# A decoder trunk on one core: the low part of each weight tile formed by an accumulating DMA instead of VectorE

## The chip, the core and the metric

The kernel runs on 1 core of one Trainium2 chip. The metric is the device time of one execution in microseconds (us); a kernel's time is the median of its runs. The engines are named as the profile names them: PE (TensorE matmul), PEld (its weight load), DVE (VectorE), ACT (ScalarE), POOL (GpSimd) and SP (SyncE, which issues DMAs here).

## What is computed

One inference step of a two-layer decoder trunk, for one prompt of 512 tokens and 8 samples of 8 tokens, which share the weights. All is float32, 1024 channels wide. In short:

```python
# layer 0: RMSNorm -> h @ w_in_e -> GLU + causal conv (31) + LayerNorm + swish, and sliding-window attention
#          -> concat @ w_out_e, added to x
# layer 1: RMSNorm -> h @ w_in_o -> causal conv (4), Mamba-2 SSD scan, gate, grouped RMSNorm -> y @ w_out_o, added to x
# behind each layer, the feed-forward part:
def conv_ffn(h, hist, w_gate, w_up, conv_w, conv_b, w_down):
    gate = h @ w_gate
    padded = jnp.concatenate([hist, gate], axis=1)
    gc = causal_dwconv(padded, conv_w, conv_b)
    y = (jax.nn.silu(gc) * (h @ w_up)) @ w_down
    return y, padded[:, -(FFN_CONV_WIDTH - 1):]
```

The outputs are the new x of both groups and the new states (convolution histories, key/value windows, SSM states).

## The kernel before

The 512 prompt tokens and 64 sample tokens stand side by side as 576 columns; channels lie on the 128 partitions. Activations are tiles of 128x576, and each product is made in two halves of 288 columns (`HALF`).

**Three products for one.** The matmuls run on operands of type float32r. To keep float32 accuracy, each operand is split into a high part, which is the value rounded to float32r, and a low part, which is the value minus the high part. `mm3` (line 152) then adds three products for each block of 128x128 weights: high weight by high activation (line 158), high weight by low activation (line 159), low weight by high activation (line 160).

**Weight tiles.** The weights come as tiles of 128x1024 (512 KB), a few as 128x896 and one as 128x256; there are 215. `weights_load` (line 137) takes a tile `wr` and loads it by a DMA on SP's queue. `weights` (line 143) then takes tiles `wh` and `wl`, makes the high part on ACT (line 148) and the low part on DVE (line 149, `wr - wh`). Each of the three tags has 3 buffers, so a tile's slot is used again three weight tiles later: `wr` once the low part has been formed, `wh` and `wl` once PE has done its last matmul with them. A 1024-wide tile feeds 48 matmuls (8 blocks, 3 products, 2 halves).

**The stages.** `mix0` is layer 0's mixer, `mix1` layer 1's with the scan `ssd`, and `ffn` comes behind each. `units` (line 243) runs a product with its evacuation per weight tile; `out_proj` (line 259) the projections that are added to x. In `ffn` weight tiles follow each other with little else on PE; in `mix0` and `mix1` PE also does transposes, attention, and small scan matmuls, while DVE and ACT do convolutions and exponentials (line 734 is a DVE step of layer 1's convolution; `acb` are tiles of decays that a DMA spreads over the partitions; line 995 is a GpSimd product on the SSM state `h`).

**What sets the order.** The tile framework schedules the program while it is built: each engine has one queue, filled in an order that the scheduler chooses from priorities and its own estimate of when inputs are there, and each instruction then waits on semaphores on the chip. GpSimd's queue before holds only small things: clearing and copying of a few columns of history (lines 296, 297, 304, 305, 722, 723, 730, 731) and the 32 products of line 995. No DMA is issued by GpSimd.

Of the kernel before, what the change touches and what calls it, by code (L numbers as in the profile page):

```python
# [6 lines left out]
F32 = mybir.dt.float32  # L7
# [3 lines left out]
ADD, SUB, MUL, MAX, MIN = ALU.add, ALU.subtract, ALU.mult, ALU.max, ALU.min  # L11
# [37 lines left out]
class Builder:  # L49
# [93 lines left out]
    def weights(self, src, n):  # L143
        nc = self.nc
        raw = self.pre.pop(0) if self.pre else self.weights_load(src, n)
        hi = self.wp.tile([P, 1024], F32R, tag="wh", bufs=3, name="wh")
        lo = self.wp.tile([P, 1024], F32R, tag="wl", bufs=3, name="wl")
        nc.scalar.activation(hi[:, :n], raw[:, :n], AF.Copy)  # L148
        nc.vector.tensor_tensor(lo[:, :n], raw[:, :n], hi[:, :n].bitcast(F32), op=SUB)  # L149
        return hi, lo  # L150

    def mm3(self, out, w, blocks, xs, sl, m=P):
# [1114 lines left out]
```

## Time and profile before

| | us |
|---|---|
| median of 2 runs | 1621.99 (1621.31 to 1622.68) |
| the profiled execution's own time | 1617.26 |
| its span in the trace | 1615.5 |
| PE busy | 1588.7 (98%) |
| PEld busy | 1504.8 (93%) |
| DVE busy | 1026.3 (64%) |
| ACT busy | 696.5 (43%) |
| POOL busy | 109.4 (7%) |

How to read it: the span is cut from the first to the last instruction of the traced execution, and its own time lies 1.8 us above it. Busy time is what an engine's instructions take; PE's matmuls are pipelined, so that one has a length of about 300 ns though the next starts 130 ns later. The share of an engine is a mean over stages with different limits, and what a change is worth is read from the stage where it falls. Idle time in the profile is put down to what ended it. "SPq" and the like are an engine's queue, where DMAs are issued.

### The profile page before, as it was taken

What the parts mean: (1) busy time and instruction counts of PE and PEld (TensorE: products, weight loads), DVE (VectorE), ACT (ScalarE), POOL (GpSimd) and SP (SyncE); (2) the same over time, 40 slices, a digit from 0 to 9 for tenths busy, and PEclk for the clock granted to TensorE, in tenths of its full rate; (3) what the DMA queues carried; (4) which work ended last, traced back from release to release, by engine and by line L of the source; (5) the groups of instructions that cost most, each with busy time, mean ns of one, the idle gap of its engine ahead of it and who ended that gap; (6) DMA issues with size and microseconds to landing.
All of it is one profiled execution on the core that took longest, in us unless ns stands there. A gap on an engine that the chain in (4) does not pass through costs nothing.

```text
span 1615.5 us, 28735 instructions
## 1 busy us (share of the span) xinstructions
PE 1588.7 (98%) x11704; PEld 1504.8 (93%) x11704; DVE 1026.3 (64%) x1847; ACT 696.5 (43%) x1333; POOL 109.4 (7%) x322
## 2 busy tenths in 40 slices
PE   8999999999999999999999999999899999999999
PEld 8996699999999999998997998998799999999999
DVE  7898677654365355578796676676776653554552
ACT  7248654322122122378766556557352221221220
POOL 0000001000000000010301101101110000000000
PEclk9999999999999999999999999999899999999999
DMA  7222022222222222224335325234222222222222
GB/s 229 71 73 69 1 66 90 80 91 79 80 90 70 93 87 76 83 72 141 132 82 166 102 70 176 92 97 156 97 69 89 91 80 79 92 71 87 92 80 76
DMA packets 63633, 150.05 MB, mean 93 GB/s; under 512 B 18558, under 2 KB 19582, under 8 KB 63502
## 3 DMA queue, kind: packets, MB, share of 16 engines
q1 hardware_dynamic: 63502, 148.23, 28.8%
q8 instruction: 92, 1.51, 0.4%
q14 instruction: 39, 0.32, 0.1%
HBM read 133.86 MB, written 14.34 MB: 92 GB/s over the span
## 4 chain that ended last, share of the span: by engine, by line
PE 89%; DVE 5%; ACT 4%; DMA 2%; issue 1%; POOL 0%; SPq 0%; DVEq 0%; ACTq 0%
PE mm L158 25%; PE mm L160 25%; PE mm L159 25%; DVE cconv L734 1%; DMA acb<-acd 1%; PE yp L974 1%; ACT wh L148 1%; PE pst L923 1%; PE po L602 1%; PE sc L581 1%; PE pt L180 1%; PE pyo L987 1%; PE yp L972 1%; PE mm L524 1%; PE pr L191 1%
## 5 line engine op out<-in xcount | busy, mean ns | idle before, releaser
L158 PE MATMUL mm<-hh,wh 128*128 128x288 f32 (+1 forms) x2288 | 680.6, 298 | 8.4 <-ACT wh L148 7.7
L160 PE MATMUL mm<-hh,wl 128*128 128x288 f32 x2288 | 679.8, 297 | 0.1
L159 PE MATMUL mm<-hl,wh 128*128 128x288 f32 (+1 forms) x2288 | 677.9, 297 | 0.0
L148 ACT ACTIVATE wh<-wr 128x1024 fp32r<-128x1024 f32 (+1 forms) x215 | 223.4, 1039 | 544.1 <-issue 283.3
L158 PEld LDWEIGHTS mm<-hh,wh 128*128 128x128 f32 (+1 forms) x2288 | 429.6, 188 | 14.8 <-ACT wh L148 8.0
L160 PEld LDWEIGHTS mm<-hh,wl 128*128 128x128 f32 x2288 | 429.7, 188 | 4.6 <-issue 2.8
L159 PEld LDWEIGHTS mm<-hl,wh 128*128 128x128 f32 (+1 forms) x2288 | 429.8, 188 | 3.5 <-issue 1.4
L149 DVE TENSOR_TENSOR wl<-wr,wh 128x1024 fp32r<-128x1024 f32 (+1 forms) x215 | 257.7, 1199 | 78.3 <-ACT wh L148 78.1
L158 PE MATMUL mm<-yh,wh 128*128 128x288 f32 x960 | 286.8, 300 | 2.5 <-ACT yh L168 2.5
L159 PE MATMUL mm<-yl,wh 128*128 128x288 f32 x960 | 287.6, 300 | 0.0
L160 PE MATMUL mm<-yh,wl 128*128 128x288 f32 x960 | 286.1, 299 | 0.0
L158 PEld LDWEIGHTS mm<-yh,wh 128*128 128x128 f32 x960 | 182.1, 190 | 6.9 <-issue 3.3
L159 PEld LDWEIGHTS mm<-yl,wh 128*128 128x128 f32 x960 | 182.1, 190 | 4.4 <-issue 3.2
L160 PEld LDWEIGHTS mm<-yh,wl 128*128 128x128 f32 x960 | 181.8, 190 | 2.9 <-issue 2.8
L257 DVE TENSOR_TENSOR x<-x,mm 128x288 f32<-128x288 f32 x192 | 85.7, 451 | 154.8 <-PE mm L160 154.4
L302 DVE TENSOR_TENSOR gbuf<-mm,rs 128x224 f32<-128x224 f32 x44 | 17.2, 392 | 108.0 <-PE mm L160 108.0
L313 ACT ACTIVATE gsilu<-gconv,par 128x512 f32<-128x512 f32 x44 | 31.8, 724 | 115.1 <-DVE gconv L310 115.1
L310 DVE SCALAR_TENSOR_TENSOR gconv<-gbuf,par,gconv 128x592 f32<-128x592 f32 x88 | 73.1, 831 | 1.5
L323 DVE TENSOR_TENSOR gsilu<-mm,gsilu 128x288 f32<-128x288 f32 x88 | 40.0, 455 | 50.3 <-PE mm L160 50.3
L683 DVE SCALAR_TENSOR_TENSOR ca<-seg,par,ca 128x576 f32<-128x576 f32 x90 | 71.3, 810 | 0.3
L734 DVE SCALAR_TENSOR_TENSOR cconv<-cbuf,par,cconv 128x600 f32<-128x600 f32 x72 | 61.4, 856 | 11.6 <-ACT cconv L732 10.6
L955 ACT ACTIVATE ew<-acb,ac 128x128 f32<-128x128 f32 x128 | 41.2, 390 | 37.4 <-DMA acb<-acd 17.6
(315 smaller groups left out, 1735.0 us busy)
## 6 DMA issues: line engine op xcount, KB each, us to landing
wr<-in_w_gate SPq DMA_DIRECT2D x44, 512.0 KB, 3.3
wr<-in_w_up SPq DMA_DIRECT2D x44, 512.0 KB, 3.3
wr<-in_w_in_o SPq DMA_DIRECT2D x40, 512.0 KB, 3.4
wr<-in_w_down SPq DMA_DIRECT2D x32, 448.0 KB, 3.3
wr<-in_w_down SPq DMA_DIRECT2D x16, 512.0 KB, 3.5
acb<-acd SPq DMA_DIRECT2D x32, 256.0 KB, 3.5
h<-in_h SPq DMA_DIRECT2D x32, 256.0 KB, 2.9
out_ssm_s<-h SPq DMA_DIRECT2D x32, 256.0 KB, 2.4
```

Source lines behind the costliest of these rows:

```text
L148: nc.scalar.activation(hi[:, :n], raw[:, :n], AF.Copy)
L149: nc.vector.tensor_tensor(lo[:, :n], raw[:, :n], hi[:, :n].bitcast(F32), op=SUB)
L158: nc.tensor.matmul(out, hi[:, ws], xh[:, sl], start=i == 0, stop=False)
L159: nc.tensor.matmul(out, hi[:, ws], xl[:, sl], start=False, stop=False)
L160: nc.tensor.matmul(out, lo[:, ws], xh[:, sl], start=False, stop=i == n - 1)
L257: nc.vector.tensor_tensor(self.x[m][:, sl], self.x[m][:, sl], p[:, :HB], op=ADD)
L310: nc.vector.scalar_tensor_tensor(cv[:, :592], g[:, k:592 + k], w(k), cv[:, :592], op0=MUL, op1=ADD)
L313: nc.scalar.activation(sl[:, :NP], cv[:, :NP], AF.Silu, bias=b)
L323: nc.vector.tensor_tensor(sl[:, HALF[half]], p[:, :HB], sl[:, HALF[half]], op=MUL)
L683: nc.vector.scalar_tensor_tensor(a, sv[:, :, k:k + 8], w, a, op0=MUL, op1=ADD)
L734: nc.vector.scalar_tensor_tensor(cv[:, :600], g[:, k:600 + k], w(k), cv[:, :600], op0=MUL, op1=ADD)
L955: nc.scalar.activation(ew[:, cs], acb[:, cs], AF.Relu, bias=ac[:, o:o + 1], scale=-1.0)
```

## The change

Two lines take the place of one, in `weights`. GpSimd writes the negated high part into `wl`, and then issues a DMA from `wr` to `wl` that adds what it brings to what is there: `-wh + wr`. The DMA goes through GpSimd's own queue, on which nothing ran before. Nothing else is edited; from here on the changed file's lines are one higher than those of before (160 becomes 161).

```diff
         nc.scalar.activation(hi[:, :n], raw[:, :n], AF.Copy)
-        nc.vector.tensor_tensor(lo[:, :n], raw[:, :n], hi[:, :n].bitcast(F32), op=SUB)
+        nc.gpsimd.tensor_scalar(lo[:, :n], hi[:, :n].bitcast(F32), -1.0, None, op0=MUL)
+        nc.gpsimd.dma_start(lo[:, :n], raw[:, :n], accum_op=ADD)
         return hi, lo
```

The scheduler then sets other orders. Three places, before and then after:

PE at the program's start, where the first two weight tiles are used (`hh` and `hl` are the parts of the activations, `wh` and `wl` those of the weights).

```order
L158 MATMUL mm<-hh,wh 128x288
L159 MATMUL mm<-hl,wh 128x288
L158 MATMUL mm<-hh,wh 128x288
L159 MATMUL mm<-hl,wh 128x288
L160 MATMUL mm<-hh,wl 128x288
L158 MATMUL mm<-hh,wh 128x288
```
```order
L159 MATMUL mm<-hh,wh 128x288
L160 MATMUL mm<-hl,wh 128x288
L159 MATMUL mm<-hh,wh 128x288
L160 MATMUL mm<-hl,wh 128x288
L159 MATMUL mm<-hh,wh 128x288
L160 MATMUL mm<-hl,wh 128x288
L161 MATMUL mm<-hh,wl 128x288
```

The first matmul with a low part was PE's fifth and is now its seventh; all behind it stands in line.

POOL in the first feed-forward part (`gbuf` is the buffer of a gate tile, `fpo` and `fso` its new history).

```order
L304 COPY fso<-gbuf 128x16
L296 MEMSET gbuf 128x2
L297 COPY gbuf<-fhist 128x8x2
L305 COPY fpo<-gbuf 128x2
L304 COPY fso<-gbuf 128x16
```
```order
L149 TENSOR_SCALAR wl<-wh 128x1024
L150 DMA wl<-wr 128x1024
L297 MEMSET gbuf 128x2
L298 COPY gbuf<-fhist 128x8x2
L149 TENSOR_SCALAR wl<-wh 128x1024
L150 DMA wl<-wr 128x1024
L306 COPY fpo<-gbuf 128x2
L305 COPY fso<-gbuf 128x16
L149 TENSOR_SCALAR wl<-wh 128x1024
```

Between GpSimd's small copies there now stands a negation with its DMA for each weight tile.

POOL in `mix1`, at the first products on the SSM state.

```order
L995 TENSOR_TENSOR h_8280<-h_8280,cds 128x512
L995 TENSOR_TENSOR h_8282<-h_8282,cds 128x512
L995 TENSOR_TENSOR h_8284<-h_8284,cds 128x512
L995 TENSOR_TENSOR h_8286<-h_8286,cds 128x512
L722 MEMSET cbuf 128x3
```
```order
L149 TENSOR_SCALAR wl<-wh 128x1024
L150 DMA wl<-wr 128x1024
L996 TENSOR_TENSOR h_8380<-h_8380,cds 128x512
L996 TENSOR_TENSOR h_8382<-h_8382,cds 128x512
L996 TENSOR_TENSOR h_8384<-h_8384,cds 128x512
L996 TENSOR_TENSOR h_8386<-h_8386,cds 128x512
L149 TENSOR_SCALAR wl<-wh 128x1024
L150 DMA wl<-wr 128x1024
```

The next tile's negation stands ahead of the four products that wait for PE, and one more behind them.

## Prediction

> **What bounds the kernel now.** I read the page first, then busy time by stage, then the chain that ended last, then the waits around the weight tiles.
>
> ```profile
> PE 1588.7 (98%) x11704; PEld 1504.8 (93%) x11704; DVE 1026.3 (64%) x1847; ACT 696.5 (43%) x1333; POOL 109.4 (7%) x322
> q1 hardware_dynamic: 63502, 148.23, 28.8%
> ```
>
> PE is busy nearly throughout; DVE, which loses work, is not the bound. The mean hides the stages, so busy time in four stretches:
>
> ```profile
> core 0: us, PE busy (x) PEld busy (x) DVE busy (x) ACT busy (x) POOL busy (x), PEclk, DMA share, GB/s
> 280.00:640.00 360.00, 360.00 (x2717) 359.79 (x2715) 191.09 (x294) 92.83 (x122) 10.25 (x62) 1.00 0.26 84
> 1200.00:1600.00 400.00, 400.00 (x3016) 399.79 (x3015) 210.99 (x326) 102.17 (x132) 14.42 (x70) 1.00 0.27 84
> 640.00:760.00 120.00, 117.64 (x863) 109.29 (x862) 85.51 (x161) 74.78 (x151) 9.36 (x26) 1.00 0.27 86
> 760.00:1160.00 400.00, 389.04 (x2944) 347.14 (x2944) 287.61 (x482) 244.89 (x499) 63.63 (x114) 1.00 0.37 122
> ```
>
> In the two feed-forward stretches, 760 us in all, PE and its weight load have no gap: 2717 matmuls in 360 us are one in 0.1325 us, so a weight tile of 48 is used up in 6.36 us. Nothing taken from DVE can shorten these. In 640 to 1160 (layer 1's mixer) PEld stands idle for 64 us of 520, and DVE is busy for 72%: only there, and in layer 0's mixer, could less DVE work help. The chain says the same: its first row below is that of 300 to 640 us, PE alone; the others are pieces of it that are DVE's low part, which are few:
>
> ```profile
> by line: PE mm L160 33.4%; PE mm L159 33.4%; PE mm L158 33.3%
> ...
> 235.47 1.23 DVE wl L149
> 242.40 1.23 DVE wl L149
> ...
> 782.49 0.76 DVE wl L149
> ```
>
> **How far ahead a weight tile is made.** Three of ACT's roundings in the feed-forward part, and the waits around them:
>
> ```profile
> 440.68 1.06 ACT L148 ACTIVATE wh<-wr 128x1024 fp32r<-128x1024 f32 x1 [4.78 <-issue]
> 447.04 1.06 ACT L148 ACTIVATE wh<-wr 128x1024 fp32r<-128x1024 f32 x1 [1.37 <-issue]
> 453.40 1.06 ACT L148 ACTIVATE wh<-wr 128x1024 fp32r<-128x1024 f32 x1 [4.73 <-issue]
> ACT wh L148 <- PE mm L159: 257.1, 72, 6.9
> DVE wl L149 <- ACT wh L148: 78.1, 111, 2.9
> SPq L139 <- DVE wl L149: 1126.6, 193, 69.1
> PE mm L158 <- ACT wh L148: 7.7, 2, 6.7
> ```
>
> ACT starts a tile every 6.36 us, when PE gives a buffer back. With three buffers, the two tiles in between still feed PE for 2 x 6.36 = 12.7 us, and that is how long a tile may take to become ready. PE waits for it only twice in the whole run.
>
> **The change part by part.** It removes 215 DVE instructions, adds 215 negations on GpSimd and 215 accumulating DMAs, and moves the release of the raw tile `wr` from DVE's end to the DMA's. The rows that price these:
>
> ```profile
> L149 DVE TENSOR_TENSOR wl<-wr,wh 128x1024 fp32r<-128x1024 f32 x182 | 222.3, 1222 | 66.5 <-ACT wh L148 66.3
> L995 POOL TENSOR_TENSOR h<-h,cds x32: 1040/1045/1881, 765.0 to 1146.3; 128x512 f32<-128x512 f32 x32
> L131 POOL MEMSET o<- 128x128 f32 x1 | 0.2, 205 | 0.0
> L127 POOL MEMSET eps<- 128x1 f32 x1 | 0.1, 99 | 0.3 <-POOLq L1237 0.3
> L731 POOL COPY cpo<-cbuf x24: 187/916/1553, 697.8 to 1071.6; 128x3 f32<-128x3 f32 x24
> L139 SPq DMA_DIRECT2D wr<-in_w_gate x44: 327/328/340, 223.9 to 1512.4; - x44
> wr<-in_w_gate SPq DMA_DIRECT2D x44, 512.0 KB, 3.3
> ```
>
> *Negation.* No row has it. From below: a memset takes (205 - 99) / 127 = 0.83 ns a column, so 1024 columns take 0.95 us. From above: GpSimd's product of two inputs takes 1045 / 512 = 2.04 ns a column, so 2.1 us. One input is half of that, and I take 1.2. Ahead of it a wait: the copies of 3 columns last 0.19 to 1.55 us, median 0.92, where DVE is busy, so I take 0.7 (0 to 1.4).
>
> *Issue.* SP needs 0.33 us for a DMA. GpSimd issued none before; between that and its longest instruction, 1.9 us, I take 1.0.
>
> *The accumulating DMA.* No row has one. A plain load of 512 KB lands in 3.3 us; at a DMA share of 0.26 a tile's load fills all 16 engines for 0.26 x 6.36 = 1.65 us, which leaves 1.65 us of fixed time. From below the accumulating one costs the same 1.65 us. From above three times that, 4.95 us, if the read of `wr`, the read of `wl` and the write go one after the other. I take twice, 3.3 us, since two bytes are read per byte written: landed 1.65 + 3.3 = 5.0 us after the issue (3.3 to 6.6). The Trainium skill, page "Collectives: The Full Stack", section "The bandwidth ceiling: the fold count and why AG ≠ RS ≠ AR", holds that a summing DMA runs at half the rate of a copy because it reads two sources, and that the addition itself costs nothing. No run shown here has one; by that page the sum would be the one that I make.
>
> *The chain from a free buffer to a ready low part*: 1.06 (ACT) + 0.7 + 1.2 + 1.0 + 5.0 + 0.1 (signals) = 9.1 us, where it was 1.06 + 1.22 + 0.1 = 2.4. That stays under 12.7, so the two feed-forward stretches cost nothing more: what hides it is the two tiles that PE still has. If that cover were gone, each tile would bring its wait. The raw tile is released 6.7 us later; its next load (0.33 + 3.3) must land within 3 x 6.36 = 19.1 us of the same start, and 9.1 + 3.6 = 12.7 does, though the load at SP's head then waits longer with what stands behind it.
>
> *Throughput.* GpSimd: 0.7 + 1.2 + 1.0 = 2.9 of 6.36 us. DMA engines in the feed-forward part: 0.26 + 2 x 0.26 = 0.78. How many tiles a stretch has is the third bracket, DVE's, in the view by stretch of the instructions on `wl`:
>
> ```profile
> core 0: us, PE busy (x) PEld busy (x) DVE busy (x), PEclk, DMA share, GB/s
> 280.00:640.00 360.00, 267.01 (x905) 169.80 (x905) 69.33 (x58) 1.00 0.26 84
> ...
> 760.00:1160.00 400.00, 208.40 (x696) 131.10 (x696) 53.75 (x44) 1.00 0.37 122
> 1200.00:1600.00 400.00, 296.43 (x1005) 188.93 (x1005) 77.39 (x65) 1.00 0.27 84
> ```
>
> Now the places where something is left.
>
> *Start.* PE's seventh instruction is now the first with a low part, and all behind it waits.
>
> ```profile
> 5.55 1.06 ACT L148 ACTIVATE wh<-wr 128x1024 fp32r<-128x1024 f32 x1
> 7.92 0.61 PE L160 MATMUL mm<-hh,wl 128*128 128x288 f32 x1
> 17.30 0.81 DVE L358 SCALAR_TENSOR_TENSOR hl<-x,par,hh 128x576 fp32r<-128x576 f32 x1
> ```
>
> It began at 7.92; rounding ends at 6.61, and 1.2 + 1.0 + 5.0 and signals put the low part at 13.9, 6.0 us later. PE was held by the arriving activations until 18.1 anyway (the last split), so part of it is made up: +4 (0 to 6).
>
> *Tiles with less notice.* By the order, nearly all tiles have 87 matmuls or more between the last use of their buffer and their first low part; ten at the seams between stages have 45 to 60, which is 6.0 to 8.0 us. Against 9.1 each would be 2.1 us late on average, 21 in all. Most lie in the mixers, where PE has longer instructions in between or waits for DVE: +6 (0 to 21).
>
> *DVE's relief and what eats it.* Two groups of DVE in 640 to 1160, and the chain of the whole run by line:
>
> ```profile
> L149 DVE TENSOR_TENSOR wl<-wr,wh 128x1024 fp32r<-128x1024 f32 (+2 forms) x59 | 70.8, 1202 | 34.4 <-ACT wh L148 34.2
> L734 DVE SCALAR_TENSOR_TENSOR cconv<-cbuf,par,cconv 128x600 f32<-128x600 f32 x72 | 61.4, 856 | 11.6 <-ACT cconv L732 10.6
> PE mm L158 25%; PE mm L160 25%; PE mm L159 25%; DVE cconv L734 1%; DMA acb<-acd 1%; PE yp L974 1%; ACT wh L148 1%; PE pst L923 1%; PE po L602 1%; PE sc L581 1%; PE pt L180 1%; PE pyo L987 1%; PE yp L972 1%; PE mm L524 1%; PE pr L191 1%
> ```
>
> DVE loses 70.8 us there, of which little was on the chain: -8 (0 to -35, half of it). Against it, a negation can hold DVE up as DVE holds up the small copies: +3 (0 to 35, 59 x 1.2 halved). The decay tiles `acb` are on the chain for 1% (16 us) and in 760 to 1160 now share the engines with 44 accumulating transfers, a DMA share of 0.37 + 44 x 3.3 / 400 = 0.73: +3 (0 to 16).
>
> **Sum.** 4 + 6 - 8 + 3 + 3 = +8 on the profiled execution's 1617.3: 1625. That execution lies 4.7 under the median of the runs shown, 1622.0, so as a median I expect 1630, slower by 0.5%. About 2% (32 us) is what a measurement of this kernel tells from no change.
>
> **The rivals.**
>
> *A: the DMA engines become the bound.* If the accumulating transfer takes three times a load or more, a tile needs 1.65 x (1 + 3) = 6.6 us of all engines and passes 6.36. That is the point from which it decides. Dense stretches hold some 143 tiles (123 in the two feed-forward ones, some 20 in layer 0's mixer). At three times: 0.24 x 143 = +34, 1664 as a median with the +8; at four times 1.89 x 143 = +270, 1900. For it: no row shows what adding in flight costs. Against it: 0.78 leaves a fifth.
>
> *B: the chain outlasts the two tiles of cover.* All upper ends together with a raw load's 1.65 in front: 1.06 + 1.4 + 2.1 + 1.9 + 6.6 + 1.65 + 0.1 = 14.8 us. Three buffers then turn over in 14.8 + 6.36, so a tile takes 7.05 us: 0.69 x 143 = +99, 1729. It decides from 12.7 us. For it: four of its six parts have no row. Against it: all must be near their upper ends.
>
> *C: negation and DVE shut each other out.* Upper ends of the lock and of `acb` without the relief: 1625 + 32 + 13 + 8 = 1678, as a median 1683; it decides once the negations take more from DVE than the 70.8 us that DVE was given. For it: the copies of 3 columns that take 0.19 to 1.55 us. The Trainium skill, page "SBUF — State Buffer", section "Who interferes with whom", states that a DVE instruction with two SBUF inputs and a GpSimd instruction that reads SBUF exclude each other for a whole instruction; these copies agree. Against it: DVE's low parts, which also had two inputs, are gone.
>
> *D: the relief is worth its upper end.* -35 in place of -8 and none of the costs: 1622 - 35 = 1587. Against it: PE was busy for 389 of 400 us there.
>
> **Chances.** Forecast 0.53, A 0.18, B 0.15, C 0.08, D 0.06. The forecast and half of C, with half its price, are within 2% (1590 to 1654): 0.57. A, B and the other half of C are slower by more: 0.37. D is faster by more: 0.06. The forecast's own range is 1610 to 1650. The range that holds 8 in 10 goes from 1605 (D left out) to 1800 (A's upper part, some 0.12, left out).
>
> **What would show it.** Right: L149 gone from DVE, DVE's busy time at about 770; in 280 to 640 and 1200 to 1600 PE still without a gap; accumulating DMAs landed some 5 us behind their issue; a DMA share of about 0.78 there. Wrong: PE's waits for `wl` in the hundreds of us. With the DMA share near 1 that is A; with gaps at every tile, free DMA engines and landings of 7 us or more it is B; longer DVE rows in 640 to 1160 are C.

## The result, and the profile after

| | us |
|---|---|
| median before (the 2 runs shown at the start) | 1621.99 |
| median after (2 runs) | 1703.21 (1702.6 to 1703.83) |
| after / before | 1.0501, 95% interval 1.0456 to 1.0546 |
| span of the profiled execution after | 1700.8 |

The change costs 5%. 1703 lies inside the predicted range (1605 to 1800), but far outside the forecast's own (1610 to 1650). That it lies in the wide range is luck: the upper part was there for rivals A and B, and neither came. Of the prediction, the account of the feed-forward parts came true; that of the start, of the seams and of the mixers did not.

The page after, busy time and queues (q0 is the queue of GpSimd's DMAs):

```profile
PE 1615.5 (95%) x11704; PEld 1522.8 (90%) x11704; DVE 865.5 (51%) x1632; ACT 699.9 (41%) x1333; POOL 876.3 (52%) x752
...
q0 software_dynamic: 30960, 110.25, 34.9%
q1 hardware_dynamic: 63502, 148.23, 27.4%
```

PE does the same 11704 matmuls. The span of the two traces grew by 85.3 us (the medians by 81). PE's idle time, which is span less busy, was 1615.5 - 1588.7 = 26.8 and is 1700.8 - 1615.5 = 85.3, so it takes 58.5 of them. The other 26.8 us are longer busy time for the same work; where most of that comes from stands further down. q0 gives the price of an accumulating tile: 0.349 x 1700.8 / 215 = 2.76 us of all 16 engines.

Busy time by stretch after (PE, PEld, DVE, ACT, POOL, granted clock, DMA share, GB/s):

```profile
280.00:640.00 360.00, 353.34 (x2639) 352.75 (x2640) 147.52 (x236) 90.74 (x118) 215.54 (x188) 0.99 0.70 163
640.00:760.00 120.00, 109.87 (x786) 104.80 (x784) 57.26 (x116) 49.77 (x92) 63.01 (x55) 0.97 0.57 134
760.00:1160.00 400.00, 374.33 (x2732) 334.42 (x2731) 230.47 (x397) 235.52 (x483) 201.65 (x188) 0.97 0.63 164
...
1300.00:1640.00 340.00, 339.85 (x2561) 339.62 (x2560) 139.60 (x223) 85.94 (x112) 207.56 (x172) 1.00 0.72 167
```

The last row lies wholly inside the second feed-forward part: no gap, 2561 matmuls in 340 us, one in 0.1328 us as before, with a DMA share of 0.72. The first row still holds some of the seam at 280 to 305. In the mixer of layer 1 PE does 2732 matmuls in the 400 us in which it did 2944.

Inside the feed-forward part, the chain of one tile (timeline after, times in us from the span's start):

```profile
445.13 1.06 ACT L148 ACTIVATE wh<-wr 128x1024 fp32r<-128x1024 f32 x1 [5.33 <-PE mm L160]
446.29 2.76 POOL L149 TENSOR_SCALAR wl<-wh 128x1024 fp32r<-128x1024 f32 x1 [2.44 <-ACT wh L148]
...
449.35 0.90 POOL L150 DMA_DIRECT2D wl<-wr  x1 [0.30 <-POOL wl L149]
```

and the median landings, counted from the start of the issue (last column, us):

```profile
wl<-wr POOLq DMA_DIRECT2D x182, 512.0 KB, 5.5
wr<-in_w_gate SPq DMA_DIRECT2D x44, 512.0 KB, 3.7
...
acb<-acd SPq DMA_DIRECT2D x32, 256.0 KB, 3.9
```

From ACT's start to the landing, with the median landing: 449.35 + 5.5 - 445.13 = 9.7 us, under the 12.7 us of the two tiles that PE still has. This tile's own DMA took 7.1 us, so 11.3 in all. Over the 109 tiles rounded in 305 to 645 and 1300 to 1640 the chain takes 9.9 us in the median and 11.5 at most, never 12.7. The run with three copies below tests that this is why these stretches lose nothing.

PE's waits after, over the whole run:

```profile
PE mm L161 <- DMA wl<-wr: 31.1, 16, 5.0
PE mm L159 <- ACT wh L148: 11.8, 3, 6.5
PE yp L975 <- DVE ew L958: 8.3, 6, 2.5
PE pyo L988 <- DMA h<-in_h: 6.0, 6, 1.5
PE pt L883 <- ACT r L862: 5.5, 1, 5.5
```

16 waits for a low part, 31 us: far from one at each of 215 tiles. To see where the time goes, compare the start of the same matmul in two traces: the k-th product with a low part (3376 in each kernel). The table gives its time before and how much later it comes in the changed kernel; the further columns are experiments told below, from their own traces.

| k, place | before | after | negation on DVE | GpSimd's instruction alone | feed-forward only | its inner tiles only | the other 85 tiles |
|---|---|---|---|---|---|---|---|
| 0, first one | 7.9 | +10.1 | +8.8 | +0.3 | +0.2 | 0.0 | +10.3 |
| 96, layer 0's mixer | 53.9 | +16.1 | +15.0 | +2.2 | +0.3 | +0.2 | +15.8 |
| 288, its end | 228.1 | +17.8 | +16.1 | +1.9 | +0.4 | +0.2 | +17.5 |
| 480, feed-forward 0 | 307.0 | +29.9 | +18.5 | +6.2 | +12.2 | +2.6 | +27.1 |
| 1344, its end | 650.8 | +30.1 | +18.4 | +6.2 | +13.3 | +3.6 | +27.2 |
| 1440, layer 1's mixer | 693.4 | +40.6 | +23.9 | +7.2 | +16.8 | +3.6 | +31.1 |
| 2304, its end | 1183.1 | +75.1 | +56.0 | +43.3 | +21.8 | +4.7 | +75.9 |
| 2400, feed-forward 1 | 1223.5 | +85.2 | +57.8 | +45.0 | +24.6 | +4.7 | +82.9 |
| 3360, end | 1605.8 | +85.3 | +57.6 | +45.0 | +24.7 | +4.7 | +82.9 |

From k = 480 to 1344 and from 2400 to 3360, that is from 307 to 651 and from 1224 to 1606, 726 us in all, the lag grows by 0.3 us. It grows by 16.1 at the start, 12.1 and 10.1 where a feed-forward part begins, 10.5 where one ends, and 34.5 in layer 1's mixer.

At the first of these seams GpSimd's rows after read:

```profile
272.79 2.77 POOL L149 TENSOR_SCALAR wl<-wh 128x1024 fp32r<-128x1024 f32 x1 [0.39 <-ACT wh L148]
275.85 0.90 POOL L150 DMA_DIRECT2D wl<-wr  x1 [0.30 <-POOL wl L149]
276.49 3.10 POOL L149 TENSOR_SCALAR wl<-wh 128x1024 fp32r<-128x1024 f32 x1
279.88 0.90 POOL L150 DMA_DIRECT2D wl<-wr  x1 [0.30 <-POOL wl L149]
```

The first tiles of the part are made half by half (`units` with a lead of 3), two roundings come 1.7 us apart (271.64 and 273.35) and not 6.36, and the second negation waits in line behind the first and its issue. The DMA issued at 279.88 lands 7.7 us later, the slowest there, and PE waits for it until 287.63.

A lost microsecond also brings a second loss. The rows of PE at that wait, and the granted clock in the two stretches behind it (columns as above):

```profile
287.63 0.61 PE L161 MATMUL mm<-hh,wl 128*128 128x288 f32 x1 [4.02 <-DMA wl<-wr]
288.04 0.44 PE L159 MATMUL mm<-hh,wh 128*128 128x288 f32 x1
288.27 0.44 PE L160 MATMUL mm<-hl,wh 128*128 128x288 f32 x1
...
293.86 0.29 PE L159 MATMUL mm<-hh,wh 128*128 128x288 f32 x1
293.99 0.29 PE L160 MATMUL mm<-hl,wh 128*128 128x288 f32 x1
```

```profile
287.60:293.60 6.00, 5.97 (x25) 5.97 (x26) 0.29 (x1) 0.00 (x0) 0.00 (x0) 0.50 0.26 88
293.70:299.00 5.30, 5.30 (x42) 5.30 (x41) 2.77 (x6) 2.34 (x2) 2.20 (x3) 1.00 0.01 3
```

Behind a wait of 4.02 us PE ran for 6 us with a granted clock of 0.50, and 0.24 us from matmul to matmul in place of 0.13: 25 matmuls that cost another 2.7 us. In the whole trace 549 matmuls start 0.20 to 0.26 us behind the one before, where there were 410; at 0.11 us each, 139 more are an estimate of 15 of the 26.8 us of longer busy time. The mean granted clock agrees with that size: 0.985 over 1700.8 us is 25.5 us short of full clock, 0.996 over 1615.5 us is 6.5 short, and part of the 19 us between them fell on an idle PE. The Trainium skill, page "TensorE: Matmul & The Clock Gate", section "HAM oscillation — how this bites in real kernels", has the rule: keep PE's idle gaps under about 3.4 us, or it falls back to half its clock and has to warm up again. The trace agrees on the half clock, but not on the length of the gap. From 37 us on (before that the clock rows read 1.00 though matmuls came 0.25 us apart, so they are left out) PE had eleven waits of over 2 us, and behind nine of them the clock was near 0.5; six of the nine were only 2.1 to 2.6 us long (the one that ended at 698.6: a mean of 0.64 over 698.6 to 702.9). Behind the other two, of 2.2 us at 304.9 and 2.1 us at 1295.5, it stayed at 1.00. Two more stretches at 0.50, at 212 and 843, stand behind no single wait of 2 us, so the length of a wait alone doesn't decide.

### The profile page after: what moved, and what is told of

Read it like the earlier page. It is cut to its first block, busy times and chain, and to the rows that moved or that the text cites. A ratio compares the mean times of both kernels' runs of the same rounds, so it can differ in the third digit from the quotient of the medians.

```text
span 1700.8 us, 29179 instructions
## 1 busy us (share of the span) xinstructions
PE 1615.5 (95%) x11704; PEld 1522.8 (90%) x11704; DVE 865.5 (51%) x1632; ACT 699.9 (41%) x1333; POOL 876.3 (52%) x752
## 5 line engine op out<-in xcount | busy, mean ns | idle before, releaser
L149 POOL TENSOR_SCALAR wl<-wh 128x1024 fp32r<-128x1024 f32 (+1 forms) x215 | 599.9, 2790 | 467.6 <-ACT wh L148 467.2
L161 PE MATMUL mm<-hh,wl 128*128 128x288 f32 x2288 | 688.2, 301 | 27.0 <-DMA wl<-wr 26.8
L159 PE MATMUL mm<-hh,wh 128*128 128x288 f32 (+1 forms) x2288 | 687.6, 301 | 12.9 <-ACT wh L148 11.8
L159 PEld LDWEIGHTS mm<-hh,wh 128*128 128x128 f32 (+1 forms) x2288 | 435.9, 191 | 21.0 <-ACT wh L148 12.4
L160 PEld LDWEIGHTS mm<-hl,wh 128*128 128x128 f32 (+1 forms) x2288 | 436.0, 191 | 2.9 <-issue 1.5
L150 POOL DMA_DIRECT2D wl<-wr x215 | 194.5, 905 | 61.7 <-POOL wl L149 54.8
L311 DVE SCALAR_TENSOR_TENSOR gconv<-gbuf,par,gconv 128x592 f32<-128x592 f32 x88 | 101.1, 1149 | 3.1
L735 DVE SCALAR_TENSOR_TENSOR cconv<-cbuf,par,cconv 128x600 f32<-128x600 f32 x72 | 68.1, 948 | 53.6 <-ACT cconv L733 52.4
L170 DVE TENSOR_TENSOR yl<-gsilu,yh 128x576 fp32r<-128x576 f32 x44 | 48.8, 1108 | 48.9 <-ACT yh L169 48.9
```

Source lines behind the costliest of these rows:

```text
L149: nc.gpsimd.tensor_scalar(lo[:, :n], hi[:, :n].bitcast(F32), -1.0, None, op0=MUL)
L150: nc.gpsimd.dma_start(lo[:, :n], raw[:, :n], accum_op=ADD)
L159: nc.tensor.matmul(out, hi[:, ws], xh[:, sl], start=i == 0, stop=False)
L160: nc.tensor.matmul(out, hi[:, ws], xl[:, sl], start=False, stop=False)
L161: nc.tensor.matmul(out, lo[:, ws], xh[:, sl], start=False, stop=i == n - 1)
L170: nc.vector.tensor_tensor(l[:, sl], src, h[:, sl].bitcast(F32), op=SUB)
```

## The experiments

Three theories stood at the beginning. **L**: the low part comes later (a chain of 9.7 us in place of 2.4), and PE waits where it has less than that in hand. **S**: the raw tile is held longer, which delays what stands on SP's queue, and the added traffic slows other transfers. **G**: GpSimd's long negation, and its lock with VectorE. Each run below was compared with the kernel before on the same chip (its medians there were 1624.3, 1619.7, 1619.6 and 1622.5 in the four groups).

**The raw tile held, without a late low part.** VectorE forms the low part as before; GpSimd copies the raw tile to a scratch in HBM.

```diff
         nc.vector.tensor_tensor(lo[:, :n], raw[:, :n], hi[:, :n].bitcast(F32), op=SUB)
+        dump = self.dp.tile([P, 1024], F32, tag="dump", bufs=3, name="dump")
+        nc.gpsimd.dma_start(dump[:, :n], raw[:, :n])
```

> The low part is made by DVE as before, and a plain DMA on GpSimd's queue then writes each raw tile out to a scratch in HBM that nobody reads: the raw tile is held until a DMA has landed, and there is a second stream of DMAs, but the low part is in time. If the 81 us come from the low part being late (L): 1622 to 1630. If they come from the raw tile being held, so that SP stands at the next load with the loads of acb and h behind it, or from the DMA traffic (S): 1660 to 1690. If they come from GpSimd's negation and its lock with DVE (G): 1622 to 1630.

Measured: 1629.14, ratio 1.0038 (1.0021 to 1.0056). The same 110 MB through GpSimd's queue (17.5% of the DMA engines' time) and a raw tile that comes free later are worth 6 us. S falls as the main cause.

**A late low part by a copy.** VectorE forms the low part; a plain DMA then copies it onto itself.

```diff
         nc.vector.tensor_tensor(lo[:, :n], raw[:, :n], hi[:, :n].bitcast(F32), op=SUB)
+        nc.gpsimd.dma_start(lo[:, :n], lo[:, :n])
```

> The low part is made by DVE as before, and a plain DMA on GpSimd's queue then copies it onto itself, so that PE gets it only when that DMA has landed; the raw tile is free as early as before. L: a chain of 1.06 + 1.22 + 0.9 + 4.5 = 7.7 us in place of 10, about 1660 to 1675. S: 1622 to 1632. G: 1622 to 1630.

Measured: 1677.47, ratio 1.0322 (1.0273 to 1.0371). The size is L's: 53 us with a late low part, the raw tile free as early as before, and as much of the DMA engines' time (18.0%) as in the run before, which cost 6. One thing more differs in these runs: where the low part is late, the scheduler also sets another order for PE. Of its 11704 places, 892 hold another matmul here than before (1349 in the change, 135 in the run before this one). What that order costs by itself no run separates; the subtraction on GpSimd, further down, bears on it.

**The negation on VectorE.** The accumulating DMA stays.

```diff
-        nc.gpsimd.tensor_scalar(lo[:, :n], hi[:, :n].bitcast(F32), -1.0, None, op0=MUL)
+        nc.vector.tensor_scalar(lo[:, :n], hi[:, :n].bitcast(F32), -1.0, None, op0=MUL)
         nc.gpsimd.dma_start(lo[:, :n], raw[:, :n], accum_op=ADD)
```

> The change with the negation on DVE in place of GpSimd: the accumulating DMA alone. L: the chain is shorter by 2.2 us, about 1670. S: nearly all of the loss stays, 1680 to 1700. G: 1622 to 1635.

Measured: 1668.65, ratio 1.0273 (1.0235 to 1.0311). L again: the DMA's part is 44 us. The two runs together also price the addition, queue and landing first of the copy:

```profile
q0 software_dynamic: 30960, 110.25, 18.0%
...
wl<-wl POOLq DMA_DIRECT2D x182, 512.0 KB, 4.8
```

and of the accumulating DMA here:

```profile
q0 software_dynamic: 30960, 110.25, 35.5%
...
wl<-wr POOLq DMA_DIRECT2D x182, 512.0 KB, 5.4
```

The same bytes take twice the engines' time (35.5% of 1673.2 against 18.0% of 1676.3 us), but land only 0.6 us later. That this run is no slower than the copy, with twice the DMA time and the raw tile held as well, speaks once more against S.

**The subtraction on GpSimd, no DMA.**

```diff
-        nc.vector.tensor_tensor(lo[:, :n], raw[:, :n], hi[:, :n].bitcast(F32), op=SUB)
+        nc.gpsimd.tensor_tensor(lo[:, :n], raw[:, :n], hi[:, :n].bitcast(F32), op=SUB)
```

> GpSimd forms the low part by itself with one subtraction of two inputs, and there is no DMA: VectorE's relief and GpSimd's lock alone. L: a chain of 1.06 + 3.5, 1620 to 1635. S: 1620 to 1635. G: 1650 to 1690.

Measured: 1721.22, ratio 1.0596 (1.0572 to 1.062): slower than all three expected, and slower than the change, although its low part is ready 1.2 us later than before and no more (2.41 us a tile against 1.20). Lateness can't explain that; two runs were then made on GpSimd's instruction alone. PE's order here is nearly that of the change (341 places differ), and yet the first product with a low part came only 1.4 us later than before, where it came 10.1 later in the change: those first 10 us at the start are not the order's.

**GpSimd's negation without its result.** VectorE forms the low part as before; behind it GpSimd negates into the raw tile, which nobody reads any more.

```diff
         nc.vector.tensor_tensor(lo[:, :n], raw[:, :n], hi[:, :n].bitcast(F32), op=SUB)
+        nc.gpsimd.tensor_scalar(raw[:, :n], hi[:, :n].bitcast(F32), -1.0, None, op0=MUL)
```

> VectorE forms the low part as before the change; behind it GpSimd does the change's own negation, of the same size, but writes it into the raw tile, which nobody reads any more; no DMA is added. It holds the raw tile some 3 us longer, which the run with the plain copy to a scratch in HBM has shown to be free. Theory G (GpSimd's long instruction and VectorE shut each other out, and that is what the change lost beyond the run with the negation on VectorE, 1703 against 1669): 1650 to 1670. Theory L (only the moment at which the low part is there counts; the change's remaining 35 us are the 2.1 us by which GpSimd's negation is longer than VectorE's, 2.77 against 0.68): 1622 to 1632, since no low part is late here.

Measured: 1658.79, ratio 1.0232 (1.0206 to 1.0259). G: 39 us with no low part late (PE has no wait for one in this trace) and no DMA added.

**The same with the two-input form.**

```diff
         nc.vector.tensor_tensor(lo[:, :n], raw[:, :n], hi[:, :n].bitcast(F32), op=SUB)
+        nc.gpsimd.tensor_tensor(raw[:, :n], raw[:, :n], hi[:, :n].bitcast(F32), op=SUB)
```

> As the run with the lock alone, but GpSimd's instruction behind VectorE's low part is the subtraction of two inputs that the run with the subtraction on GpSimd had (1721), written into the raw tile that nobody reads any more. Theory G: the two-input form shuts VectorE out for longer (there the 592-column steps of VectorE took 1803 ns against 831), so 1690 to 1740, above the one-input form. Theory L: 1622 to 1635; the 1721 would then come from the 1.2 us by which the subtraction on GpSimd is later than on VectorE.

Measured: 1734.76, ratio 1.0707 (1.0686 to 1.0727). G, and with it the 1721. PE's order is the same in this run and the last, so it isn't what sets them apart; and the run with the subtraction on GpSimd, in nearly the order of the change, lost less than this one. Four groups show how (behind the first bar busy us and mean ns of one, behind the second the idle time ahead): GpSimd's instruction; two VectorE steps that read two tiles from SBUF, `gconv` in the feed-forward parts and `cconv` in layer 1's mixer; and one that reads one of its two from PSUM (`x<-x,mm`). Before, VectorE's (the row of `cconv`, 856 ns, stands in the prediction); then beside GpSimd's negation; then beside its subtraction:

```profile
L257 DVE TENSOR_TENSOR x<-x,mm 128x288 f32<-128x288 f32 x192 | 85.7, 451 | 154.8 <-PE mm L160 154.4
L310 DVE SCALAR_TENSOR_TENSOR gconv<-gbuf,par,gconv 128x592 f32<-128x592 f32 x88 | 73.1, 831 | 1.5
```

```profile
L150 POOL TENSOR_SCALAR wr<-wh 128x1024 f32<-128x1024 f32 (+1 forms) x215 | 649.6, 3022 | 653.5 <-DVE wl L149 544.3 <-issue 68.7 <-ACT zs L1033 20.0
...
L311 DVE SCALAR_TENSOR_TENSOR gconv<-gbuf,par,gconv 128x592 f32<-128x592 f32 x88 | 101.0, 1147 | 1.5
L258 DVE TENSOR_TENSOR x<-x,mm 128x288 f32<-128x288 f32 x192 | 85.5, 451 | 154.4 <-PE mm L161 154.1
...
L735 DVE SCALAR_TENSOR_TENSOR cconv<-cbuf,par,cconv 128x600 f32<-128x600 f32 x72 | 72.3, 1007 | 10.8 <-ACT cconv L733 9.0 <-POOL cpo L732 0.5
```

```profile
L150 POOL TENSOR_TENSOR wr<-wr,wh 128x1024 f32<-128x1024 f32 (+1 forms) x215 | 568.7, 2646 | 743.8 <-DVE wl L149 607.1 <-issue 82.6 <-ACT zs L1033 20.5
...
L311 DVE SCALAR_TENSOR_TENSOR gconv<-gbuf,par,gconv 128x592 f32<-128x592 f32 x88 | 160.4, 1823 | 1.5
...
L735 DVE SCALAR_TENSOR_TENSOR cconv<-cbuf,par,cconv 128x600 f32<-128x600 f32 x72 | 99.9, 1391 | 12.6 <-ACT cconv L733 11.4
...
L258 DVE TENSOR_TENSOR x<-x,mm 128x288 f32<-128x288 f32 x192 | 85.2, 450 | 145.2 <-PE mm L161 144.9
```

The steps with two SBUF inputs grow, `gconv` from 831 to 1147 and 1823 ns, `cconv` from 856 to 1007 and 1391; the one that reads PSUM stays at 451. So VectorE is not slower as a whole: it is held up where it reads two tiles from SBUF. GpSimd's one-input form is the longer instruction of the two, and yet holds VectorE up less. The feed-forward parts lose nothing by their longer `gconv`; 36 of the 45 us that the run with the negation loses in the table lie in layer 1's mixer. There GpSimd's own queue is a rival: VectorE waited 29.1 us for the products on `h` that GpSimd makes, before 17.5. In the two-input run it waited 16.3 us for them and the loss was far larger, so the queue is not its cause; how the negation's 36 us divide between the two is not shown. In the changed kernel itself `cconv` grew less:

```profile
L735 DVE SCALAR_TENSOR_TENSOR cconv<-cbuf,par,cconv 128x600 f32<-128x600 f32 x72 | 68.1, 948 | 53.6 <-ACT cconv L733 52.4
```

**Only the feed-forward parts, behind their first three tiles.** 130 tiles go the change's way, VectorE does the rest.

```diff
+        if self.dma_lo:
             nc.gpsimd.tensor_scalar(lo[:, :n], hi[:, :n].bitcast(F32), -1.0, None, op0=MUL)
             nc.gpsimd.dma_start(lo[:, :n], raw[:, :n], accum_op=ADD)
+        else:
+            nc.vector.tensor_tensor(lo[:, :n], raw[:, :n], hi[:, :n].bitcast(F32), op=SUB)
...
         self.units([G(f) for f in range(lead)], lead)
+        self.dma_lo = True
```

> The change's way (negation on GpSimd, accumulating DMA) for 130 of the 215 weight tiles, those of the two feed-forward parts behind their first three tiles; VectorE forms the low part of the 85 others as before. Theory L with the cover of two tiles (in the feed-forward parts PE still has 12.7 us of work while a tile is made, and the chain takes 9.8): 1622 to 1637. Rival theory P (each of these transfers costs its share of the 81 us wherever it stands, by load on the DMA engines or by GpSimd): 130/215 of 81 us, about 1673.

Measured: 1642.36, ratio 1.014 (1.0122 to 1.0157). Between the two, nearer to L. The table says where: +11.8 at its entry into the first part, in one wait of 7.97 us and what follows it, then 1.1 in 340 us. GpSimd's rows there tell of a cause that no theory had:

```profile
270.31 2.80 POOL L151 TENSOR_SCALAR wl<-wh 128x1024 fp32r<-128x1024 f32 x1 [0.22 <-ACT wh L149]
...
276.83 0.68 POOL L309 COPY fso<-gbuf 128x16 f32<-128x16 f32 x1 [2.86 <-DVE gbuf L308]
277.46 0.48 POOL L310 COPY fpo<-gbuf 128x2 f32<-128x2 f32 x1
277.91 2.76 POOL L151 TENSOR_SCALAR wl<-wh 128x1024 fp32r<-128x1024 f32 x1
280.62 1.94 POOL L152 DMA_DIRECT2D wl<-wr  x2
```

The first tile's negation ends at 273.1, but its DMA goes out only at 280.6: small copies of the gate's history, one of which waits for VectorE's `gbuf`, and the second tile's negation stand between the two on GpSimd's queue. In the changed kernel itself that is rare: there 203 of 215 DMAs go out within 0.6 us of their negation, and the 12 others lose 11 us together.

**Without these tiles.** The same, with VectorE also for the first seven tiles of each part and the last eight: 106 tiles are left.

```diff
             for f in range(a, b):
+                self.dma_lo = f > 1
...
             last = b == NF
+            self.dma_lo = not last
```

> As the run with the change's way in the feed-forward parts alone (1642, against 1620), but without the tiles next to their seams: VectorE also forms the low parts of the first seven weight tiles of each part and of its last eight, so that GpSimd and the accumulating DMA do some 106 of 215. In the run before, nearly all of the 23 us were lost at 270 to 290, 670 to 710 and 1230 us, where the products of three or four tiles are made half by half, so that their buffers come free nearly together. Theory L with the cover: 1617 to 1627, since the 9.8 us of the chain lie under two whole tiles of 6.36 us everywhere. Rival P (each accumulating transfer costs its share wherever it is): 106/130 of 23 us, about 1639.

Measured: 1623.66, ratio 1.0021 (1.0009 to 1.0033). L: 106 negations and accumulating DMAs, half of the change, cost some 3 us, and one of them again stood 6.3 us behind its negation where the way changes. This is also the fastest version with the DMA found here. None of the versions beats the kernel before, where PE already is busy for 98% of the span.

**The other 85 tiles.** The start, both mixers and the first three tiles of each feed-forward part go the change's way, the 130 don't (the flag of the run before last, turned round).

> The complement of the run with the change's way in the feed-forward parts alone: GpSimd and the accumulating DMA make the low part of the other 85 weight tiles (the start, the two mixers and the first three tiles of each feed-forward part), VectorE that of the 130. Theory L with the cover, and G: the losses belong to places and add up, so the change's 81 us less the 23 us of that run: 1620 + 58 = 1678 (1665 to 1695). Rival P (by the number of tiles): 1620 + 85/215 of 81 = 1652. If the relief of VectorE in the mixers is worth anything, it is in this run too.

Measured: 1699.73, ratio 1.0474 (1.045 to 1.0497), 80 us: these 85 tiles bear the whole loss. It is more than the 58 expected: the losses of the two halves, 80 and 23 us, don't add up to the change's 81. About half of the other run's loss (11.8 us in the table) was that one DMA behind the copies and the second negation, which neither this kernel nor the change has; the rest of the difference was not followed. The rival by number of tiles falls, and VectorE's relief in the mixers shows no gain.

**Three copies in a row.** The cover tested from the other side.

```diff
         nc.vector.tensor_tensor(lo[:, :n], raw[:, :n], hi[:, :n].bitcast(F32), op=SUB)
+        nc.gpsimd.dma_start(lo[:, :n], lo[:, :n])
+        nc.gpsimd.dma_start(lo[:, :n], lo[:, :n])
+        nc.gpsimd.dma_start(lo[:, :n], lo[:, :n])
```

> VectorE forms the low part as before, and three plain DMAs, one behind the other, then copy it onto itself. The chain from a rounded tile to a ready low part is 2.4 + 3 x (0.3 + 4.8) = 17.7 us, above the 12.7 us of the two tiles of cover. Theory L with the cover: in the feed-forward parts a tile takes (17.7 + 6.36) / 3 = 8.0 us in place of 6.36, so 123 x 1.66 = 204 us more, and at the seams and in the mixers three times the 53 us of the run with one copy, or more: 1960 to 2060, with a gap at every tile of the feed-forward parts. Rival (the cover has nothing to do with it, each copy costs its 53 us wherever it is): 1624 + 159 = 1783, feed-forward parts without gaps.

Measured: 2046.68, ratio 1.2637 (1.2594 to 1.268). L with the cover. The first feed-forward stretch of this kernel, and PE's largest wait in it:

```profile
280.00:640.00 360.00, 306.66 (x2099) 299.80 (x2098) 164.09 (x271) 87.02 (x129) 85.50 (x201) 0.92 0.76 252
```

```profile
PE mm L163 <- DMA wl<-wl: 52.1, 23, 7.4
```

2099 / 48 = 43.7 tiles in 360 us, 8.2 us each, where (17.7 + 6.36) / 3 = 8.0 was expected. 23 waits for 44 tiles, so not a gap at every tile; 52 us of waits and a clock of 0.92 make up the stretch's loss.

**The start on VectorE.** The change, but for the first eight tiles.

```diff
+        self.made += 1
+        if self.made > 8:
             nc.gpsimd.tensor_scalar(lo[:, :n], hi[:, :n].bitcast(F32), -1.0, None, op0=MUL)
             nc.gpsimd.dma_start(lo[:, :n], raw[:, :n], accum_op=ADD)
+        else:
+            nc.vector.tensor_tensor(lo[:, :n], raw[:, :n], hi[:, :n].bitcast(F32), op=SUB)
```

> The change, but for the first eight weight tiles, whose low parts VectorE forms as before. In the changed kernel PE is 16 us behind after the first 96 products with a low part and loses nothing more until layer 0's mixer ends. Theory L (the low part is late because nothing has been prepared yet; the losses of the places add up): 1703 - 16 = 1687 (1680 to 1692). Rival (that lag is made up anyway by waits further on): 1700 to 1706.

Measured: 1693.94, ratio 1.045 (1.0417 to 1.0482), neither: in its trace the lag at k = 96 is 0.0, so the 16 us of the start are all gone, but from there to the end it loses 74.5 us, where the change lost 69.2. Some 9 of 16 us stay won. Most of the difference (5 us) arises in layer 1's mixer; which waits grow there was not followed.

**The negation on ScalarE.**

```diff
-        nc.gpsimd.tensor_scalar(lo[:, :n], hi[:, :n].bitcast(F32), -1.0, None, op0=MUL)
+        nc.scalar.activation(lo[:, :n], hi[:, :n].bitcast(F32), AF.Copy, scale=-1.0)
         nc.gpsimd.dma_start(lo[:, :n], raw[:, :n], accum_op=ADD)
```

> The change, with the negation on ScalarE (ACT), right behind its rounding and of the same length, 1.06 us; the accumulating DMA stays on GpSimd's queue. No long instruction on GpSimd, none of VectorE's shared inputs. The chain is 1.06 + 1.06 + 0.3 + 5.4 = 7.8 us, where it was 7.6 with the negation on VectorE (1669) and 9.8 with the negation on GpSimd (1703). Theory L and G together (lateness of the low part, plus GpSimd's and VectorE's lock, which is gone): 1660 to 1678. Theory L alone with the slope of those two runs, 34 us for 2.2 us of chain: 1672, so that this run doesn't tell them apart, but says whether VectorE's relief, here complete and without any lock, is worth something: then under 1660. If ACT, whose steps are on the mixers' chain too, becomes the bound there: over 1680.

Measured: 1665.59, ratio 1.0261 (1.0232 to 1.029). As with VectorE's negation. VectorE, busy for 799 us and without a long instruction of GpSimd beside it, brings nothing that shows in return; but ACT is busy for 895 us here in place of 699, and what that takes away is not separated.

**The account.** Medians against before: the accumulating DMA without GpSimd's negation +44, GpSimd's negation without the DMA +39, both (the change) +81. Over the whole run that adds up. Place by place it adds up less well: in layer 1's mixer the two alone lose 32 and 36 us, the change 34.5, while at the seams the change loses more than the two together. That the totals add up is therefore partly chance. Beside the run with VectorE's negation the change loses 2 us more in layer 1's mixer and 23 more at the three seams, so what GpSimd's negation adds in the change lies mostly at the seams, where its chain is 2 us longer and negations stand in line. The run with GpSimd's negation alone also holds the raw tile longer; by the first experiment up to 6 of its 39 us may be that.

## Why the prediction was right and wrong

The forecast, 1630, was wrong by 73 us, and the range held by luck. Rival A asked for three times a load's engine time, and it was 1.7 times. Rival B asked for a chain over 12.7 us, and in the feed-forward parts it was 11.5 at most. C, with the nearest price (1683), had a chance of 0.08, and it names one part of the loss. The steps of the sum, one by one:

- **The cover: right.** The chain was put at 9.1 us: "That stays under 12.7, so the two feed-forward stretches cost nothing more". It was 9.7 with the median landing, and they lost 0.3 us; with 17.7 the period became 8.2 us.
- **The DMA's price: nearly right.** Landing 5.0 forecast, 5.5 measured; engine time 3.3 forecast (twice a load), 2.76 measured (1.7 times); DMA share 0.78 forecast, 0.72 measured. Against a plain copy from SBUF to SBUF it is twice (35.5% against 18.0%). The page of the Trainium skill that is cited there, "Collectives: The Full Stack", gives this factor for reduce-scatter against all-gather; the trace agrees for a DMA within SBUF.
- **The negation: wrong, outside its bounds.** The step that failed: "One input is half of that, and I take 1.2." It took 2.8 us (599.9 us for 215). A form of one input is not half a form of two here: 3.02 us without the DMA, against 2.65 for the two-input subtraction. In the chain this was made up by a shorter wait ahead and a quicker issue (0.9).
- **The start: wrong size.** +4 (0 to 6) forecast, +16 measured. The negation ran from 6.57 to 9.34, and the transfer, issued at 9.65 beside the loads of activations and weights (the profile puts the DMA engines' share at 1.09, so all taken, over 12 to 18), was used at 17.98, 8.3 us later in place of 5.0. The other 6 of the 16 us came behind it, among them one more wait of 2.1 us for a low part at 37.5; nothing of that was in the term.
- **Tiles with less notice: wrong size.** The step: "Most lie in the mixers, where PE has longer instructions in between or waits for DVE: +6 (0 to 21)." The three seams alone took 33 us; in layer 1's mixer the run with VectorE's negation, without GpSimd's, lost 32. That PE has something in between did not help: in the change it waited for `ew`, `h` and `r` as well (8.3, 6.0 and 5.5 us), not only for `wl`. That these came late because the products ahead of them did is argued, not shown.
- **The clock: left out.** Most waits of over 2 us were followed by a stretch at half clock, by the estimate above some 15 us in all. The prediction priced a wait at its length.
- **The relief of VectorE: not seen.** -8 (0 to -35) forecast; between the runs with VectorE's and ScalarE's negation VectorE's busy time differs by 126 us (925.5 and 799.0), and their ratios are 1.0273 and 1.0261. That ACT bears the negation in the second keeps this from being a clean test.
- **The lock: wrong size, as far as it can be told.** +3 (0 to 35) forecast; GpSimd's negation by itself cost 39. Rival C described this mechanism, and said how it would show: longer VectorE rows in 640 to 1160. They are there (`cconv` 856 ns before, 948 after), but half of that growth stands also in the run with VectorE's negation (907). VectorE's busy time fell to 865.5, not to the forecast 770; with the negation on ACT, where it has the same 1632 instructions, it was 799.0, so beside GpSimd's negation they took 66 us longer. How much of that reached the end is not shown: in layer 1's mixer the change loses only 2 us more than the run with VectorE's negation. "DVE's low parts, which also had two inputs, are gone" was no protection of VectorE's time: the convolutions and products that remain have two inputs as well. C's price, 1683, was made without the late low parts.
- **`acb`: not settled.** ACT waited 54.5 us for these tiles, 17.6 before, and 36 with VectorE's negation; PE's waits don't show how much of that reached the end.

So the forecast failed in sizes that were taken low (the start, the tiles with less notice, GpSimd's negation), and in one multiplier that was missing. What it said would prove it wrong, waits for `wl` in the hundreds of us, was the wrong sign to watch: they were 31 us of 81.

## What to carry to other kernels

A buffer ring hides a longer chain only where tiles are used up one after the other; count the notice at the start, at seams and in stages that interleave halves, because there the excess is paid, and PE's slow restart behind most longer waits is paid on top. An instruction that is moved to GpSimd can be paid for by VectorE's steps with two SBUF inputs: with the subtraction on GpSimd VectorE was busy for 1055 us, before 1026, although all its low parts were gone. Price those steps, by stage, before counting on an idle GpSimd. An engine that is busy for 64% need not give anything back when it is relieved.

## What the runs showed of the hardware

- Adding in flight doubled a DMA's engine time (35.5% against 18.0% of the span for the same 110 MB), and lengthened its landing only from 4.8 to 5.4 us and GpSimd's issue from 0.53 to 0.86 us (medians).
- GpSimd's negation of 128x1024 took 2.8 to 3.0 us, its subtraction of two such inputs 2.4 to 2.6 us.
- Under GpSimd's long instructions VectorE's `gconv` step with two SBUF inputs grew in the mean from 831 to 1147 ns (negation) and 1823 ns (subtraction); a step with one input in PSUM stayed at 451 ns.
- PE restarted at a granted clock of 0.50 behind a wait of 4 us, and kept it for 6 us. From 37 us on, nine of eleven waits of over 2 us were followed by about half clock, six of them shorter than 2.7 us.
